# Gate and residual for the first half of an output projection, and gates stored tile by tile

## The chip, the cores and the metric

The kernel runs on one core of a Trainium2 chip. The metric is the time of one execution on the device, in microseconds (us). The kernel before took 3386.41 us, the median of three runs from 3386.09 to 3387.73.

## The reference

One step of a diffusion backbone with two kinds of linear recurrence side by side, in fp32. There are 2048 latent tokens (a grid of 64 columns and 32 rows) and 128 context tokens, of 1024 features each.

```python
def _layer(x, mod, st_a, st_b, p, grid_rows):
    sh1, sc1, g1, sh2, sc2, g2 = split(mod)
    h = rms_norm(x, norm1) * (1 + sc1) + sh1
    # group A, HGRN2 in raster order; group B, gated DeltaNet in column order
    o_a = head_rms_norm(oa_f + flip(oa_b)) * silu(a_g)
    o_b = head_rms_norm(ob_f + flip(ob_b)) * silu(b_z)
    y = concat([o_a, o_b]) @ w_out          # (tokens, 1024) x (1024, 1024)
    x = x + g1 * y                          # g1 is one row for latent, one for context tokens
    h = rms_norm(x, norm2) * (1 + sc2) + sh2
    return x + g2 * ((silu(h @ w_gate) * (h @ w_up)) @ w_down), states
```

Since `concat([o_a, o_b]) @ w_out` is a sum of two products, `x + g1 * y` can be taken as `(x + g1 * (o_a @ w_a)) + g1 * (o_b @ w_b)` or as `x + g1 * (o_a @ w_a + o_b @ w_b)`.

## The kernel before

Tokens are handled in 17 tiles of 128: 16 of latent tokens, in column order of the grid, and one of the context (index `NL`). fp32 products are made of three products of split halves (`oh`, `ol` and `woh`, `wol`). The stages come in this order: norm and transposes; the input projections, the short convolution and the two sigmoid gates; the HGRN scan; the preparation of the gated DeltaNet scan; the gated DeltaNet scan itself, with the output projection worked into it; the FFN.

Four pieces of work matter here.

*The gates.* `gate_block` (L268 to L280) computes one head's gate for all 2176 tokens, with the head's 128 features on partitions, in one tile `ct`, and stores it to `gate_d` in DRAM. There are eight such blocks, four heads for each of the two groups. `out_a` (L790) loads back one tile's gates of four heads (L802).

*The triangular inverse.* For the DeltaNet scan a 128x128 triangular matrix of each tile and head is inverted: 32x32 blocks on VectorE and GpSimd, and then two levels on TensorE, in `A3` (L650 to L705). One tile's levels are a chain of small matmuls (L675, L681, L686, L696, L701) with copies on ScalarE and VectorE between them. The result lies in one of two buffers `XT` and is stored by L705. The latent tiles come first, the context tile last. The memory of these work tiles is given back when the last tile is done, and later ones (`g1c` among them) are laid out over it.

*The scan.* `scan` (L914) takes one tile in one direction: matmuls `pkS`, `pv`, `pS`, `po`, `pa`, of which each depends on the one before through VectorE or ScalarE. 34 steps are run, 16 latent tiles and the context in both directions. `scan_load` (L886) and `scan_pre` (L898, whose product is `pqk`, L905) prepare a step.

*The output projection.* It is made in two parts: part 0 is the HGRN group's share, for which everything is there early, part 1 the DeltaNet group's, for which a tile must have been passed by both directions of the scan. For each tile and part `out_a` norms the heads, transposes them (L820) and applies the gate (L821 to L823); `out_b` (L826) makes two halves of 512 output features, each with 12 matmuls into a PSUM tile `py` (L847), of which there are two. In part 0 the half is copied (L855) and the sum parked in DRAM (`xa_d`, L857). In part 1 it is added to what was parked (L851, VectorE), multiplied by the gate row `gm` (L852, GpSimd), added to the residual x (L853, GpSimd) and stored to `x2_d` (L859). The gate row is `g1`, held all the time, for latent tiles, and `g1c`, loaded when needed, for the context tile (L836). `out_step` calls both one after the other for each tile; part 0 begins with the context tile, part 1 takes it among its first tiles.

The order of instructions on each engine is not that of the source. A scheduler that simulates a timeline fixes it when the program is built (`schedule_with_timeline_sim=True`), so each engine has a static order, and an instruction that must wait holds back all that stand behind it on its engine. All DMAs are issued by SyncE (SP), also in one static order.

Of the kernel before, what the change touches and what calls it, by code (L numbers as in the profile page):

```python
# [24 lines left out]
H = 4  # L25
# [8 lines left out]
def hybrid_step(ctx: ExitStack, tc, x, vecs, ada1, ada2, bada, win, wgt, alog, dtb, sa, sb, wout, wg, wu, wd, normf,  # L34
# [19 lines left out]
    def scr(shape, name):  # L54
        return drm.tile(shape, F32, tag=name, name=name)


    qkv_d = scr([NT, P, 4, H, P], "qkvd")
    gate_d = [scr([P, H, TOK], f"gated{i}") for i in range(2)]
    oa_d = scr([TOK, H, P], "oad")  # L60
    mod_d = scr([2, 4 * D], "modd")
    gr_d = scr([2, NT * H, P], "grd")
# [205 lines left out]
    def gate_block(b):  # L268
        w = load_w(win[16 + b if b < H else 32 + b - H])
        ct = gq.tile([P, TOK], F32, tag="gct", name="gct")  # L270
        for i, (c0, n) in enumerate(PIECES):
            pj = proj(w, i)
            r0, r1 = lat_rows(i)
            nl = (r1 - r0) * GW
            nc.scalar.activation(out=colmajor(ct[:, 0:LAT])[:, r0:r1, :],
                                 in_=pj[:, 0:nl].rearrange("p (r c) -> p r c", c=GW), func=AF.Copy)
            if nl < n * P:
                nc.scalar.activation(out=ct[:, LAT:TOK], in_=pj[:, nl:n * P], func=AF.Copy)
        nc.scalar.activation(out=ct, in_=ct, func=AF.Silu)
        dma(out=gate_d[b // H][:, b % H, :], in_=ct)  # L280


    with sB:
# [470 lines left out]
    def rows_of(src, c, w):  # L754
        return src[0:LAT].rearrange("(r w) f -> w r f", w=GW)[4 * c + w]
# [34 lines left out]
    def out_a(c, part, ob):  # L790

        o4 = ob
        if part == 0:
            o4 = wk5.tile([P, H, P], F32, tag="o4", name="o4", bufs=3)
            oaf = oa_d.rearrange("t h v -> t (h v)")
            if c == NL:
                dma(out=o4.rearrange("p h v -> p (h v)"), in_=oaf[LAT:TOK])
            else:
                for w in range(4):
                    dma(out=o4[32 * w:32 * w + 32].rearrange("p h v -> p (h v)"), in_=rows_of(oaf, c, w))  # L800
        gt = wk5.tile([P, H, P], F32, tag="gt5", name="gt5", bufs=3)
        dma(out=gt, in_=gate_d[part][:, :, c * P:(c + 1) * P])  # L802
        sq = wk5.tile([P, 3, H], F32, tag="sq5", name="sq5", bufs=10)
        jk = wk5.tile([P, P], F32, tag="jk5", name="jk5")
        for h in range(H):
            nc.scalar.activation(out=jk, in_=o4[:, h], func=AF.Square, accum_out=sq[:, 0, h:h + 1])  # L806
        if part == 0:
            nc.vector.tensor_scalar(out=sq[:, 0], in0=sq[:, 0], scalar1=1.0 / P, scalar2=EPS, op0=ALU.mult,
                                    op1=ALU.add)
        else:  # L810
            nc.vector.scalar_tensor_tensor(out=sq[:, 0], in0=sq[:, 0], scalar=1.0 / P, in1=nq2[:, c],
                                           op0=ALU.mult, op1=ALU.add)
        rsqrt(sq[:, 1], sq[:, 0], sq[:, 2])
        for h in range(H):
            nc.scalar.activation(out=o4[:, h], in_=o4[:, h], func=AF.Copy, scale=sq[:, 1, h:h + 1])
        oh = wk5.tile([P, H, P], F32R, tag="oh", name="oh", bufs=2)
        ol = wk5.tile([P, H, P], F32R, tag="ol", name="ol", bufs=2)
        pt = ps5.tile([P, H, P], F32, tag="ot", name="ot")
        for j in range(H):
            nc.tensor.transpose(pt[:, j], o4[:, j], ident)  # L820
        nc.vector.tensor_tensor(out=gt, in0=pt, in1=gt, op=ALU.mult)  # L821
        nc.scalar.activation(out=oh, in_=gt, func=AF.Copy)
        nc.vector.tensor_tensor(out=ol, in0=gt, in1=oh, op=ALU.subtract)  # L823
        return oh, ol

    def out_b(c, part, oh, ol):  # L826

        xt = wk5.tile([P, D], F32, tag="xt5", name="xt5", bufs=2)
        gm = g1
        if part:  # L830
            x2 = wk5.tile([P, D], F32, tag="x2", name="x2", bufs=2)
            dma(out=xt, in_=xa_d[c])
            if c == NL:
                dma(out=x2, in_=x[LAT:TOK])
                gm = wk6.tile([P, D], F32, tag="h2", name="g1c")
                dma(out=gm, in_=mod_d[1:2, 0:D].broadcast_to([P, D]))  # L836
            else:
                for w in range(4):
                    dma(out=x2[32 * w:32 * w + 32], in_=rows_of(x, c, w))
        woh, wol = wos[part]  # L840
        for n in range(2):
            cs = slice(512 * n, 512 * n + 512)
# [2 lines left out]
            for k in range(H):  # L845
                for a, b in ((oh, woh), (oh, wol), (ol, woh)):
                    nc.tensor.matmul(out=py, lhsT=a[:, k], rhs=b[:, k, cs], start=t == 0,  # L847
                                     stop=t == 3 * H - 1)
                    t += 1
            if part:  # L850
                nc.vector.tensor_tensor(out=xt[:, cs], in0=py, in1=xt[:, cs], op=ALU.add)  # L851
                nc.gpsimd.tensor_tensor(out=xt[:, cs], in0=xt[:, cs], in1=gm[:, cs], op=ALU.mult)  # L852
                nc.gpsimd.tensor_tensor(out=x2[:, cs], in0=x2[:, cs], in1=xt[:, cs], op=ALU.add)  # L853
            else:
                nc.vector.tensor_copy(out=xt[:, cs], in_=py)  # L855
        if not part:
            dma(out=xa_d[c], in_=xt)  # L857
            return None
        dma(out=x2_d[c], in_=x2)  # L859
        return x2  # L860

    def norm_T(c, xt, h2, r, bank):

# [526 lines left out]
```

## Time and profile before

| What | Value |
|---|---|
| Median of three runs | 3386.41 us |
| The profiled execution: its time, its span | 3381.0 us, 3379.1 us |
| Mean granted TensorE clock in it | 0.965 |
| Busy: PE, DVE, ACT, POOL | 3148.7, 1877.4, 1388.1, 987.8 us |
| Levels of the inverse (L650 to L705) end | 1463 us after the span's start |
| Projection part 0, matmuls | 1325 to 1533 us |
| Projection part 1, matmuls of latent tiles | 1619 to 1833 us |
| First FFN matmul (L1169) | 1846 us |

Times of the trace are counted from the span's start. "Busy" is the time in which an engine had an instruction running; overlapping matmuls are counted once in a stretch's busy time, while the groups of the same matmuls add up their durations. "PEclk" is the clock granted to TensorE as a share of full speed. A wait is put down to the engine and instruction that released it last.

### The profile page before, as it was taken

The page shows a single profiled execution, that of the slowest core. Times are in us where ns is not written, and L with a number is a line of the kernel's source. Part 1 is how long each engine was busy: PE and PEld are TensorE (multiplying, and loading weights), DVE is VectorE, ACT ScalarE, POOL GpSimd, SP SyncE. Part 2 cuts the span into 40 slices and gives each one's busy share as a digit, 9 for nine tenths or more (in the row PEclk, how much of TensorE's full clock was granted, in tenths as well). Part 3 has the DMA queues.
Part 4 walks back from the last instruction along what each step waited for, and adds up shares of the span by engine and source line. Part 5 has one row for each costly group of instructions (what it writes and reads, how often), then busy time and mean ns, then how long its engine had stood idle before and what let it go on. Part 6 is the DMA issues. An engine that isn't in the chain of part 4 may idle for free.

```text
span 3379.1 us, 50825 instructions
## 1 busy us (share of the span) xinstructions
PE 3148.7 (93%) x18712; PEld 2815.3 (83%) x18712; DVE 1877.4 (56%) x3702; ACT 1388.1 (41%) x2993; POOL 987.8 (29%) x1006
## 2 busy tenths in 40 slices
PE   7899979999999889998886999998999999999997
PEld 4687779999998777878775888987999998899996
DVE  4667744474563864665666777778233337333336
ACT  6455435364474534763753545543111113211111
POOL 1100001121122327413566444456111114211114
PEclk8999999999999988999998999998999999999998
DMA  5234410111115667867775888988656666666553
GB/s 219 71 111 142 116 54 29 53 47 36 49 42 150 170 171 247 275 226 264 250 243 168 343 339 334 352 342 322 223 192 218 218 210 233 248 218 218 208 200 116
DMA packets 325241, 647.85 MB, mean 192 GB/s; under 512 B 77178, under 2 KB 177314, under 8 KB 310146
## 3 DMA queue, kind: packets, MB, share of 16 engines
q1 hardware_dynamic: 324994, 644.61, 56.2%
q8 instruction: 148, 2.42, 0.3%
q14 instruction: 99, 0.81, 0.1%
HBM read 446.23 MB, written 198.28 MB: 191 GB/s over the span
## 4 chain that ended last, share of the span: by engine, by line
PE 43%; DVE 6%; DMA 5%; ACT 3%; POOL 2%; issue 2%; SPq 0%; POOLq 0%; DVEq 0%; ACTq 0%
PE z L1169 23%; PE y L1252 12%; PE py L847 3%; PE pS L938 1%; PE pj L257 1%; DVE wp L1067 1%; DMA e<-grd 1%; PE pa L954 1%; DMA wr<-in_wu_dram 1%; DVE acc L1204 1%; DMA x<-in_x_dram 1%; PE po L947 0%; DVE acc L1257 0%; POOL s L1070 0%; ACT jk L806 0%
## 5 line engine op out<-in xcount | busy, mean ns | idle before, releaser
L257 PE MATMUL pj<-hh,wh 128*128 128x384 f32 (+2 forms) x1480 | 546.9, 370 | 14.3 <-DVE q L464 7.0
L257 PE MATMUL pj<-hl,wh 128*128 128x384 f32 (+2 forms) x1480 | 545.9, 369 | 0.4 <-POOL hl L231 0.3
L257 PE MATMUL pj<-hh,wl 128*128 128x384 f32 (+2 forms) x1480 | 545.6, 369 | 0.0
L1316 POOL TENSOR_TENSOR u<-u,g 128x384 f32<-128x384 f32 (+1 forms) x132 | 135.9, 1031 | 779.0 <-DVE u L1177 758.5
L1257 DVE TENSOR_TENSOR acc<-y,acc 128x512 f32<-128x512 f32 x328 | 223.9, 688 | 251.4 <-PE y L1252 250.8
L257 PEld LDWEIGHTS pj<-hh,wh 128*128 128x128 f32 (+1 forms) x1480 | 281.1, 190 | 46.6 <-DVE q L464 7.2
L257 PEld LDWEIGHTS pj<-hl,wh 128*128 128x128 f32 (+1 forms) x1480 | 280.7, 190 | 29.9 <-issue 3.3
L257 PEld LDWEIGHTS pj<-hh,wl 128*128 128x128 f32 (+1 forms) x1480 | 280.6, 190 | 28.0 <-issue 2.3
L1252 PE MATMUL y<-wd,hid0h 128*128 128x512 f32 x748 | 237.7, 400 | 19.7 <-DVE acc L1257 7.2
L1252 PE MATMUL y<-wd,hid1h 128*128 128x512 f32 x748 | 236.6, 397 | 0.8 <-DMA wd<-wdd 0.8
L1295 ACT ACTIVATE g<-g 128x384 f32<-128x384 f32 (+1 forms) x132 | 66.6, 507 | 288.5 <-DVE g L1177 288.4
L494 POOL TENSOR_SCALAR th<-th,nlbh,lbh 128x384 f32<-128x384 f32 (+1 forms) x40 | 61.2, 1530 | 405.7 <-ACT G L492 401.8
L1252 PEld LDWEIGHTS y<-wd,hid0h 128*128 128x128 f32 x748 | 137.5, 190 | 41.7 <-DVE acc L1257 9.3
L1252 PEld LDWEIGHTS y<-wd,hid1h 128*128 128x128 f32 x748 | 140.8, 189 | 32.5 <-issue 1.2
L1177 DVE TENSOR_TENSOR g<-z,g 128x384 f32<-128x384 f32 (+1 forms) x165 | 85.1, 533 | 146.7 <-PE z L1169 146.1
L1169 PE MATMUL z<-x1h,wp 128*128 128x384 f32 (+1 forms) x528 | 143.7, 335 | 17.9 <-ACT wp L1066 13.2
L1169 PE MATMUL z<-x6h,wp 128*128 128x384 f32 (+1 forms) x528 | 145.9, 334 | 14.2 <-ACT wp L1066 8.6
L1177 DVE TENSOR_TENSOR u<-z,u 128x384 f32<-128x384 f32 (+1 forms) x165 | 84.9, 531 | 117.9 <-PE z L1169 117.5
L1252 PE MATMUL y<-wd,hid1l 128*128 128x512 f32 x374 | 147.4, 397 | 1.7 <-POOL hid1l L1067 1.7
L1252 PE MATMUL y<-wd,hid0l 128*128 128x512 f32 x374 | 148.0, 399 | 0.0
L1066 ACT ACTIVATE hid1h<-u 128x384 fp32r<-128x384 f32 (+3 forms) x77 | 34.2, 458 | 267.7 <-POOL u L1316 267.7
L1169 PE MATMUL z<-x2h,wp 128*128 128x384 f32 (+1 forms) x528 | 140.8, 329 | 1.1 <-DMA wp<-wpd 1.1
(373 smaller groups left out, 7904.6 us busy)
## 6 DMA issues: line engine op xcount, KB each, us to landing
wp<-wpd SPq DMA_DIRECT2D x308, 512.0 KB
wpd<-wp SPq DMA_DIRECT2D x154, 512.0 KB
wd<-wdd SPq DMA_DIRECT2D x44, 1024.0 KB
ld<-qkvd SPq DMA_DIRECT2D x34, 1024.0 KB
wdd<-wd SPq DMA_DIRECT2D x22, 1024.0 KB
raw<-in_win_dram SPq DMA_DIRECT2D x72, 256.0 KB
e<-grd SPq DMA_DIRECT2D x68, 256.0 KB
at<-in_ada_dram SPq DMA_DIRECT2D x64, 256.0 KB
```

The source lines that it names most:

```text
L257: nc.tensor.matmul(out=out, lhsT=a[:, k], rhs=b[:, k], start=t == 0, stop=t == 3 * KD - 1)
L494: nc.gpsimd.tensor_scalar(out=th, in0=th, scalar1=nlbh[:, col:col + 1], scalar2=lbh[:, col:col + 1], op0=ALU.mult, op1=ALU.add)
L847: nc.tensor.matmul(out=py, lhsT=a[:, k], rhs=b[:, k, cs], start=t == 0, stop=t == 3 * H - 1)
L938: nc.tensor.matmul(out=pS[:, h], lhsT=kn[:, h], rhs=vv[:, h], start=True, stop=True)
L954: last[0] = nc.tensor.matmul(out=pa[:, h], lhsT=at[:, h], rhs=vv[:, h], start=True, stop=True)
L1066: nc.scalar.activation(out=wh, in_=raw, func=AF.Copy)
L1169: nc.tensor.matmul(out=z, lhsT=w_[:, k], rhs=x_[:, k, :N], start=t == 0, stop=t == 3 * HK - 1)
L1177: nc.vector.tensor_tensor(out=out, in0=z, in1=b, op=ALU.add)
L1252: nc.tensor.matmul(out=py, lhsT=u_[:, o:o + P], rhs=v_[:, cs], start=t == 0, stop=t == 5)
L1257: nc.vector.tensor_tensor(out=acc[c][:, cs], in0=py, in1=acc[c][:, cs], op=ALU.add)
L1295: nc.scalar.activation(out=g, in_=g, func=AF.Silu)
L1316: nc.gpsimd.tensor_tensor(out=us[i], in0=us[i], in1=gs[i], op=ALU.mult)
```

## The change

Two things are changed. The gates are stored as one block for each tile (`gate_d` has the tile as its first index): the store of a gate block writes 17 pieces of 512 bytes for each partition in place of one row of 8.7 KB, and the load of a tile's gates reads one piece of 2 KB in place of four of 512 bytes. And `out_b` does in both parts what it did in neither before: it multiplies the half by the gate row straight out of PSUM (VectorE) and adds to it (GpSimd) what stands in `xt`, which is the residual x in part 0 and the parked sum in part 1.

```diff
-    gate_d = [scr([P, H, TOK], f"gated{i}") for i in range(2)]
+    gate_d = [scr([NT, P, H, P], f"gated{i}") for i in range(2)]
...
-        dma(out=gate_d[b // H][:, b % H, :], in_=ct)
+        dma(out=gate_d[b // H][:, :, b % H, :].rearrange("c p t -> p c t"), in_=ct.rearrange("p (c t) -> p c t", t=P))
...
-        dma(out=gt, in_=gate_d[part][:, :, c * P:(c + 1) * P])
+        dma(out=gt, in_=gate_d[part][c])
...
     def out_b(c, part, oh, ol):
 
         xt = wk5.tile([P, D], F32, tag="xt5", name="xt5", bufs=2)
+        x2 = wk5.tile([P, D], F32, tag="x2", name="x2", bufs=2)
         gm = g1
+        if c == NL:
+            gm = wk6.tile([P, D], F32, tag="h2", name="g1c")
+            dma(out=gm, in_=mod_d[1:2, 0:D].broadcast_to([P, D]))
         if part:
-            x2 = wk5.tile([P, D], F32, tag="x2", name="x2", bufs=2)
             dma(out=xt, in_=xa_d[c])
-            if c == NL:
-                dma(out=x2, in_=x[LAT:TOK])
-                gm = wk6.tile([P, D], F32, tag="h2", name="g1c")
-                dma(out=gm, in_=mod_d[1:2, 0:D].broadcast_to([P, D]))
-            else:
-                for w in range(4):
-                    dma(out=x2[32 * w:32 * w + 32], in_=rows_of(x, c, w))
+        elif c == NL:
+            dma(out=xt, in_=x[LAT:TOK])
+        else:
+            for w in range(4):
+                dma(out=xt[32 * w:32 * w + 32], in_=rows_of(x, c, w))
...
-            if part:
-                nc.vector.tensor_tensor(out=xt[:, cs], in0=py, in1=xt[:, cs], op=ALU.add)
-                nc.gpsimd.tensor_tensor(out=xt[:, cs], in0=xt[:, cs], in1=gm[:, cs], op=ALU.mult)
-                nc.gpsimd.tensor_tensor(out=x2[:, cs], in0=x2[:, cs], in1=xt[:, cs], op=ALU.add)
-            else:
-                nc.vector.tensor_copy(out=xt[:, cs], in_=py)
-        if not part:
-            dma(out=xa_d[c], in_=xt)
-            return None
-        dma(out=x2_d[c], in_=x2)
-        return x2
+            nc.vector.tensor_tensor(out=x2[:, cs], in0=py, in1=gm[:, cs], op=ALU.mult)
+            nc.gpsimd.tensor_tensor(out=x2[:, cs], in0=x2[:, cs], in1=xt[:, cs], op=ALU.add)
+        dma(out=(xa_d, x2_d)[part][c], in_=x2)
+        return x2 if part else None
```

The change also moves instructions on every engine. Lines behind L826 differ between the two files: L847, L905, L927, L933 and L889 of before are L848, L899, L921, L927 and L883 of after.

On PE, in the middle of the inverse's levels. `pl` and `pn` are the levels' products (L675 to L701), `py` the projection's, `pqk`, `pkS` and `pa` the scan's. Before:

```order
L847 MATMUL py<-woh,ol 128x512
L701 MATMUL pl_10429<-kTa 64x64 x8
L681 MATMUL pl_10462<-NS,dd 32x32 x16
L847 MATMUL py<-woh,oh 128x512
L847 MATMUL py<-wol,oh 128x512
```

After, at the same levels:

```order
L820 MATMUL ot<-ident,o_12405 128x128 x4
L696 MATMUL pl_10429<-XT_8657,e 64x64 x8
L675 MATMUL pl_10462<-dd,L 32x32 x16
L899 MATMUL pqk<-ld 128x128 x4
L948 MATMUL pa<-vv,e 128x128 x4
L921 MATMUL pkS<-S_12833,ld 128x128
L701 MATMUL pl_10429<-kTa 64x64 x8
L681 MATMUL pl_10462<-NS,dd 32x32 x16
L921 MATMUL pkS<-S_12833,ld 128x128 x3
L686 MATMUL pn_10496<-dd,NS 32x32 x4
```

Between the context tile's two halves and the last level, before has 18 further halves of `py` (216 matmuls), after none; before has come to 14 tiles of L820 by the last level, after to 7. Both have done six scan steps by then. Behind the last level, the halves of part 0 that are left stand among five scan steps before, and 34 halves among seven after; the steps that follow up to the twentieth, nine before and seven after, have no projection beside them in either.

On SP, where the levels end. `xtd` is the store of a tile's inverse, `XT<-xtd` the scan's load of it, `g1c` the context's gate row, `wor` weights of the output projection, `xad` the parked sum. Before:

```order
L705 DMA xtd<-XT_8656 128x1024
L800 DMA o_14468<-oad 32x512
L892 DMA XT<-xtd 128x512 x3
L836 DMA g1c<-modd 128x1024
L892 DMA XT<-xtd 128x512
L783 DMA wor<-in_wout_dram 128x1024
L857 DMA xad_12203<-xt_13255 128x1024
```

After:

```order
L705 DMA xtd<-XT_8656 128x1024
L705 DMA xtd<-XT_8657 128x1024
L705 DMA xtd<-XT_8656 128x1024
L833 DMA g1c<-modd 128x1024
L886 DMA XT<-xtd 128x512 x3
L833 DMA g1c<-modd 128x1024
L886 DMA XT<-xtd 128x512
L853 DMA xad_12216<-x_12370 128x1024
L840 DMA xt_12510<-in_x_dram 32x1024 x4
```

The first load of the gate row stands at the same place as the only one before, behind the store of the last tile's inverse; a second one follows for part 1. Of the parked sums nine (the first of them far ahead of these rows) are stored before that place in the kernel before, and none in the kernel after.

On DVE, at the same place of the kernel after. L704 and L690 end a tile's levels, and `g1c` is read by the first output of the projection:

```order
L704 COPY XT_8657<-pl_10921 64x4x64 x2
L690 COPY XT_8656<-pl_10954 32x4x32 x4
L688 COPY NS<-pn_10988 32x4x32 x2
L704 COPY XT_8656<-pl_11003 64x4x64 x2
L923 SCALAR_TENSOR_TENSOR ld<-pkS,nrg,ld 128x128 x4
L851 TENSOR_TENSOR x_12370<-py,g1c 128x512 x2
L851 TENSOR_TENSOR x_12440<-py,g_12282 128x512 x2
```

Before, the copies of L855 that take their place stand among the levels of eight tiles, the first of them behind L820 of the third tile.

## Rows read from the trace of the kernel before

**Rows 1.** The page, parts 1 and 4: busy us (share) xinstructions; chain by engine.

```profile
span 3379.1 us, 50825 instructions
PE 3148.7 (93%) x18712; PEld 2815.3 (83%) x18712; DVE 1877.4 (56%) x3702; ACT 1388.1 (41%) x2993; POOL 987.8 (29%) x1006
...
PE 43%; DVE 6%; DMA 5%; ACT 3%; POOL 2%; issue 2%; SPq 0%; POOLq 0%; DVEq 0%; ACTq 0%
```

**Rows 2.** Windows: us; PE, PEld, DVE, ACT, POOL busy; PEclk; DMA; GB/s.

```profile
1333.00:1463.00 130.00, 125.39 (x1342) 107.71 (x1341) 77.12 (x218) 86.99 (x281) 54.75 (x91) 0.96 0.83 273
1463.00:1610.00 147.00, 127.29 (x832) 113.98 (x829) 75.42 (x191) 68.93 (x187) 42.22 (x46) 0.95 0.76 255
1540.00:1610.00 70.00, 56.09 (x439) 53.75 (x438) 35.86 (x107) 32.59 (x94) 26.98 (x30) 0.95 0.82 278
1612.00:1818.00 206.00, 185.17 (x1131) 159.76 (x1130) 138.93 (x355) 129.30 (x374) 121.48 (x104) 0.97 0.71 229
1818.00:1846.00 28.00, 10.82 (x28) 7.40 (x28) 22.59 (x22) 10.02 (x21) 22.68 (x15) 0.68 0.37 131
```

**Rows 3.** PE groups from 1330 to 1465: shapes xcount | busy us, mean ns.

```profile
L847 PE MATMUL py<-woh,oh 128*128 128x512 f32 x76 | 31.1, 409 | 0.0
L820 PE MATMUL ot<-ident,o 128*128 128x128 f32 x48 | 7.7, 277 | 0.0
```

**Rows 4.** L847, two halves: ns, first and last start of every third matmul.

```profile
L847 PE MATMUL py<-woh,oh x8: 390/394/479, 1405.7 to 1410.7; 128*128 128x512 f32 x8
```

**Rows 5.** SP's issue of the context gate, L836.

```profile
L836 SPq DMA_DIRECT2D g1c<-modd x1: 319/319/319, 1470.6 to 1470.6; - x1
```

**Rows 6.** SP: stores of the level results, L705.

```profile
L705 SPq DMA_DIRECT2D xtd<-XT x11: 320/377/1818, 1302.9 to 1466.2; - x11
```

**Rows 7.** Two neighbouring tiles in the levels, L696.

```profile
L696 PE MATMUL pl<-XT,e x16: 218/218/313, 1301.6 to 1302.3; 64*64 64x64 f32 x16
L696 PE MATMUL pl<-XT,L x16: 311/311/365, 1310.0 to 1311.3; 64*64 64x64 f32 x16
```

**Rows 8.** The scan steps without projection, L938 (8 matmuls each).

```profile
L938 PE MATMUL pS<-vv,ld x72: 275/275/582, 1548.1 to 1611.3; 128*128 128x128 f32 x72
```

**Rows 9.** DMA from 1333 to 1463.

```profile
DMA packets 28782, 35.44 MB, mean 273 GB/s; under 512 B 12288, under 2 KB 20621, under 8 KB 27609
```

**Rows 10.** PE's waits from 1612 to 1818.

```profile
PE pS L938 <- ACT vv L935: 7.6, 8, 3.0
PE ot L820 <- POOL x L853: 4.2, 3, 1.9
PE nt L870 <- DVE h L873: 2.3, 2, 1.9
PE py L847 <- ACT oh L822: 1.8, 2, 1.2
PE ot L820 <- POOL xt L852: 1.3, 1, 1.3
```

**Rows 11.** POOL groups from 1612 to 1840.

```profile
L852 POOL TENSOR_TENSOR xt<-xt,g 128x512 f32<-128x512 f32 x32 | 41.8, 1308 | 40.5 <-DVE xt L851 14.9 <-DVE sq L127 6.8 <-DVE sq L131 6.3
L853 POOL TENSOR_TENSOR x<-x,xt 128x512 f32<-128x512 f32 x32 | 41.5, 1300 | 6.7 <-PE ot L820 2.2 <-DMA x<-in_x_dram 1.8 <-PE py L847 0.8
```

**Rows 12.** DVE: L823 from 1465 to 1541, without additions on POOL.

```profile
L823 DVE TENSOR_TENSOR ol<-gt,oh 128x512 fp32r<-128x512 f32 x6 | 4.1, 686 | 0.7 <-ACT oh L822 0.7
```

**Rows 13.** DVE: L823 and L128 from 1612 to 1834, beside them.

```profile
L823 DVE TENSOR_TENSOR ol<-gt,oh 128x512 fp32r<-128x512 f32 x16 | 12.8, 803 | 0.9 <-ACT oh L822 0.9
...
L128 DVE TENSOR_TENSOR sq<-sq 128x4 f32<-128x4 f32 (+1 forms) x19 | 9.1, 480 | 0.4
```

**Rows 14.** Windows within one store: 512 B pieces, then 8.7 KB rows.

```profile
301.00:303.00 2.00, 2.00 (x13) 2.00 (x12) 0.69 (x1) 1.87 (x11) 0.00 (x0) 1.00 1.05 291
...
1071.00:1073.00 2.00, 1.15 (x9) 0.76 (x8) 0.00 (x0) 1.44 (x6) 1.64 (x2) 1.00 1.08 442
```

**Rows 15.** PE's waits from 1818 to 1850.

```profile
PE z L1169 <- ACT wp L1066: 13.2, 1, 13.2
```

## The prediction

> **What bounds the kernel now.** I read the page first. PE is busy for 3148.7 of the span's 3379.1 us, and the chain that ended last lies more on PE than on anything else [rows 1]. So the kernel is bound by how densely PE's work stands in its static order, and time is won or lost only where PE stands idle. I then cut the stretch that the change touches into windows [rows 2]. From 1333 to 1463 us, while the inverse's levels run, PE is busy for 125.4 of 130 us: the small matmuls of the levels are chains of waits, and projection and scan fill their gaps. From 1463 to 1610 us PE has 127.3 of 147, and in its second part, where only scan steps are left, 56.1 of 70. The nine steps there start their `pS` from 1548.1 to 1609.7 us or so (72 matmuls in nine groups of eight, the last at 1611.3 [rows 8]), 7.7 us each. In part 1 (1612 to 1818) PE has 185.2 of 206. The waits of PE there name GpSimd's L852 and L853 and what comes late through ScalarE and VectorE [rows 10]. Last come 28 us with 10.8 of PE, which end with a wait of 13.2 us for the FFN's first weights [rows 2, 15].
>
> **The change, part by part.** The sum is made against the profiled execution, 3381.0 us with 1.9 us around its span; it is 5.4 us under the median of 3386.4 us, and I add that at the end.
>
> *Work is kept, and moved.* 34 copies and 34 additions on VectorE become 68 multiplications that also read one PSUM and one SBUF tile. GpSimd keeps 68 operations, of which 34 move from part 1 to part 0; each took 1.30 us [rows 11]. The 8.9 MB of x are now read in part 0. Only the second load of `g1c` is new, 0.5 MB.
>
> *Term 1, the levels.* This is the part of the change that its text does not tell. In part 0 the first half of the projection now needs the gate row of the context. Its load stood at 1470.6 us, directly behind the last store of the inverse at 1466.2 [rows 5, 6], and stands at the same place after; but before, part 0 did not ask for it. With two PSUM tiles for `py`, no third half can be made until then, and the order on PE shows just that: the 18 halves are gone from between the levels, and with them 7 tiles of L820. One half is 12 matmuls; the 24 of two halves ran from 1405.7 to 1411.5 at 0.238 us each (21 steps in 5.0 us [rows 4]), so 2.85 us a half and 51 us for 18. The other two thirds of the 229 recorded matmuls have rows like the one in [rows 3]. Seven tiles of L820 are 28 transposes at most 0.28 us apart [rows 3] and overlapped; I take half, 4 us. So PE loses 55 of its 125 us of work, and 70 are left. How far does the stretch shrink? Three things hold it up. The chain of one tile, unfilled, took 8.4 us (1301.6 to 1310.0 [rows 7]); eight tiles make 67. Six scan steps at 7.7 make 46 beside them; run one after the other with the levels that would be 113. And the DMAs moved 35.4 MB here at 273 GB/s [rows 9]; without nine parked sums, two weight loads and the inputs of seven tiles (10 MB) about 26 MB are left, 95 us at this rate. The last three stores of the inverse stand back to back, with nothing beside them on SP. I take 100 us, a little above the DMAs' 95, since both chains share one in-order PE: −30. Bounds: −60 (only the 70 us of PE's work count) and 0 (SP and the two chains hold it where it was).
>
> *Term 2, the work comes back.* The 55 us stand behind the levels. The first output waits for `g1c` and the x tiles behind it on SP: +3 (0 to +6). Seven scan-only steps in place of nine leave PE two times less idle; nine had 13.9 us [rows 2], so −3. 34 additions of GpSimd now run beside this part. They were seen to slow VectorE: L823 took 686 ns without them and 803 beside them, and the little operations of L128 took 480 ns on average there [rows 12, 13]. Most of that hides behind 34 dense halves; +2 (0 to +10). DMA is no bound: 37.5 MB of this stretch (147 us at 255 GB/s) and 10.5 more in some 203 us are 236 GB/s, less than the 273 seen before. Sum +57, bounds +48 to +70.
>
> The Trainium skill, "SBUF — State Buffer", section "Who interferes with whom", says that VectorE with two inputs in SBUF and GpSimd reading SBUF share a port pair, which one holds for a whole instruction while the other is fully blocked. The rows agree: an operation of four elements lasted as long as a good part of an addition. By this rule the blocking moves into part 0 with the 34 additions and leaves part 1 by as much, and the new multiplication, with only one input in SBUF, is not touched; the sum stays what it is.
>
> *Term 3, part 1.* Each tile loses two of four operations on GpSimd and 512 KB of x loads in SP's queue. PE's 5.5 us of waits for L852 and L853 should go, and half of the 11.7 us for L935, L873 and L822, which are late through blocked VectorE or a late `ld` [rows 10]: −11. Bounds 0 (a scan step's own latency takes their place) and −21 (all idle time of the stretch [rows 2]).
>
> *Term 4, the end.* The last two halves pass one operation of GpSimd in place of two: −2.6, bounds −4 and 0, since the 13.2 us of waiting for the FFN's weights [rows 15] are mostly these weights' own.
>
> *Term 5, the gate layout.* Eight stores become pieces of 512 B. A store of the same size with such pieces ran at 291 GB/s, the row-wise one at 442 [rows 14]; 1.11 MB take 3.8 in place of 2.5 us. That makes 10 us of DMA time, while PE works on the next block; the 34 loads gain about as much. I take 0, bounds −3 and +10. The Trainium skill, "DMA: Bandwidth & Descriptors", section "Specifications", puts line rate at pieces of 512 B and up, by which the store would cost nothing more; the trace does not agree, with 291 beside 442 GB/s. By either the sum is the same.
>
> Sum: −30 + 57 − 11 − 2.6 + 0 = +13, so 3394 us for an execution like the profiled one and 3399 us on the median's footing.
>
> **The rivals.**
>
> *Faster: the levels close up.* If steps and levels overlap well and the DMAs run as fast as within one store, 291 to 442 GB/s [rows 14], the stretch falls to its 72 us of PE's work: −58 + 56 − 14 − 3 = −19, and 3367 us. For it: the levels need little DMA. Against it: 26 MB in 72 us are 360 GB/s, where 273 was the mean.
>
> *No change.* The stretch falls to 88 us and part 1 gains a little more: −42 + 56 − 13 − 2 = −1, about 3385 us. For it: work is only moved. Against it: moved from where PE's gaps are to where they are fewer.
>
> *Much slower.* Scan steps and levels run one after the other on PE's in-order queue, 113 us, and wait for loads behind a blocked SP besides, 120: −10 + 60 − 8 − 2 = +40, about 3426 us. What decides is where the last level ends: behind 1448 us this is the case. For it: 4.6 us of idle time were all that the fillers left, so latency of the chains was hidden and its real size is not seen.
>
> *The change does not do what it says:* if blocked GpSimd or VectorE keep part 1 at its 13.7 us a step (206 us for 15 steps), term 3 is 0 and the time 3410 us. This lies inside the forecast's own bounds.
>
> **How the numbers follow.** What a measurement of this kernel can tell from no change is about 0.2%, 7 us. Forecast and its neighbours (3393 to 3412 us): 0.38. Much slower: 0.12. No change: 0.20. Faster: 0.30; it has so much because every term's bound below is far from what I took. Slower is therefore 0.50, same 0.20, faster 0.30. The likeliest case alone reaches from 3390 to 3414 us; the range for 8 times in 10 takes in the faster case and most of the much slower one, 3364 to 3426 us.
>
> **What would show it.** In the profile after: no `py` between about 1333 us and the last L701, whose end I expect near 1433 us (right between 1420 and 1448; below 1410 the faster rival, above it the slower one). The first multiplication with `g1c` about 3 us later, and PE waiting there for DMA or VectorE. Scan-only steps of 7.7 us, seven of them. The first projection matmul of a latent tile in part 1 near 1646 us in place of 1619. Part 1 at 13.0 us a step in place of 13.7, with GpSimd's L852 named less often by PE's waits. L823 slower than 686 ns in the dense part, nearer to 690 in part 1. A gate store at about 290 GB/s. The forecast is wrong if this matmul comes before 1630 us, or if part 1 keeps its step.

## The result and the profile after

The changed kernel took 3422.22 us, the median of four runs from 3420.36 to 3423.36, beside 3386.25 us for the kernel before (four runs, 3384.17 to 3387.73): slower by 36 us, or 1.0106 by these eight times. The ratio on record is 1.0119, with a 95% interval from 1.0100 to 1.0139 that holds both. The forecast had 3399 us, slower by 13: the direction was right, the size was not.

The two profiled executions differ by 42.4 us of span (3379.1 and 3421.5). I cut both at the same points of the program:

| Stretch, from PE's matmuls | Before, us | After, us | Difference | Forecast |
|---|---|---|---|---|
| to the first of the projection | 1325.3 | 1329.1 | +3.8 | 0 |
| on to the last of the levels (L701) | 137.8 | 116.4 | −21.4 | −30 |
| on to the twentieth scan step | 146.6 | 209.7 | +63.1 | +57 |
| on to the 34th scan step (part 1) | 199.0 | 199.0 | 0.0 | −11 |
| on to the FFN's first | 37.5 | 36.1 | −1.4 | −2.6 |
| the FFN's | 1518.9 | 1518.1 | −0.8 | 0 |

The rows add up to 43.3 us; the tail behind the FFN's last matmul was 0.9 us shorter after. The forecast's terms add up to +13.4. A scan step is counted from its first `pS`. The cuts are read from the first and last starts of a line's instructions. Of the kernel after: the last levels, the loads of the context's gate row (two now), the scan steps up to the twentieth, and the FFN's first group.

```profile
L701 PE MATMUL pl<-NS x64: 218/218/365, 1364.6 to 1445.5; 64*64 64x64 f32 x64
...
L833 SPq DMA_DIRECT2D g1c<-modd x2: 319/319/319, 1449.6 to 1455.2; - x2
...
L932 PE MATMUL pS<-vv,ld x60: 275/275/553, 1596.3 to 1656.8; 128*128 128x128 f32 x60
...
L1163 PE MATMUL z<-x1h,wp x528: 302/334/689, 1890.2 to 3349.1; 128*128 128x384 f32 x117, 128*128 128x320 f32 x59
```

The gate row is asked for 21 us earlier than before [rows 5], because the levels end 18 us earlier, and the twentieth step's last `pS` comes at 1656.8 in place of 1611.3 [rows 8]. What was won in the levels is lost three times over behind them.

The windows of the kernel after that answer to [rows 2] (same columns; the cuts are those of the table):

```profile
1329.00:1445.00 116.00, 89.34 (x1156) 80.02 (x1154) 58.02 (x170) 69.74 (x220) 58.32 (x99) 0.83 0.81 250
1445.00:1655.00 210.00, 182.13 (x1063) 157.38 (x1060) 103.97 (x249) 89.16 (x255) 82.51 (x74) 0.94 0.80 256
1655.00:1854.00 199.00, 180.33 (x1100) 158.27 (x1100) 129.92 (x344) 127.27 (x363) 83.60 (x75) 0.95 0.57 195
...
1863.00:1892.00 29.00, 11.80 (x31) 7.98 (x31) 22.20 (x21) 12.35 (x27) 21.08 (x14) 0.67 0.37 134
```

In the levels PE is idle for 27 us, where 4.6 us were idle before, and the granted clock is 0.83 in place of 0.96. In part 1 the columns of GpSimd and of the DMAs show the relief that was made: GpSimd down from 121 of 206 us to 84 of 199, DMA from 0.71 to 0.57. PE's columns show that it bought nothing.

PE's waits of the kernel after, first in the levels (1336 to 1446):

```profile
PE pqk L899 <- DMA ld<-qkvd: 7.0, 1, 7.0
PE pkS L921 <- ACT of L957: 5.1, 1, 5.1
PE ot L820 <- ACT o L815: 4.8, 2, 3.6
PE pl L696 <- ACT XT L668: 2.7, 4, 1.5
```

behind them (1446 to 1594):

```profile
PE py L848 <- DVE x L851: 7.8, 5, 3.6
PE pv L927 <- DMA XT<-xtd: 2.4, 1, 2.4
```

and in part 1 (1655 to 1854):

```profile
PE pS L932 <- ACT vv L929: 14.6, 9, 4.4
PE nt L864 <- ACT x L858: 4.6, 3, 2.3
PE py L848 <- ACT oh L822: 1.5, 3, 0.9
PE ot L820 <- POOL x L852: 0.7, 1, 0.7
```

The waits for GpSimd's L852 and L853 were 5.5 us [rows 10] and are 0.7. In their place stands the wait for `vv`, a copy on ScalarE. ScalarE's timeline of the kernel after shows what stood ahead of one such wait of 2.74 us (start, length, instruction; `pv` was done by 1747.7; the last line is PE's):

```profile
1748.17 1.28 ACT L898 ACT_TABLE_LOAD   x1
1749.46 1.28 ACT L898 ACTIVATE e<-e,nG 128x128 f32<-128x128 f32 x4
1750.65 0.57 ACT L929 ACTIVATE vv<-pv 128x512 f32<-128x512 f32 x1
1751.27 0.94 PE L932 MATMUL pS<-vv,ld 128*128 128x128 f32 x6 [2.74 <-ACT vv L929]
```

ScalarE does not wait here; it is busy with the next step's exponentials, and the table load for them, which stand ahead of `vv` in its static order. In the kernel before they stood there too, ahead of a wait of 2.98 us:

```profile
1709.30 1.28 ACT L904 ACT_TABLE_LOAD   x1 [0.29 <-DMA e<-grd]
1711.33 1.28 ACT L904 ACTIVATE e<-e,nG 128x128 f32<-128x128 f32 x4 [0.74 <-POOL e L900]
1712.51 0.58 ACT L935 ACTIVATE vv<-pv 128x512 f32<-128x512 f32 x1
1713.14 1.16 PE L938 MATMUL pS<-vv,ld 128*128 128x128 f32 x8 [2.98 <-ACT vv L935]
```

There 0.74 us of ScalarE's time were a wait for GpSimd, so before the change a part of this delay came from GpSimd after all.

### The profile page after: what moved, and what is told of

Read it like the earlier page. It is cut to its first block, busy times and chain, and to the rows that moved or that the text cites. A ratio compares the mean times of both kernels' runs of the same rounds, so it can differ in the third digit from the quotient of the medians.

```text
span 3421.5 us, 50857 instructions
## 1 busy us (share of the span) xinstructions
PE 3160.7 (92%) x18712; PEld 2824.5 (83%) x18712; DVE 1873.7 (55%) x3702; ACT 1390.7 (41%) x2995; POOL 987.4 (29%) x1006
## 4 chain that ended last, share of the span: by engine, by line
PE 39%; DVE 6%; ACT 4%; DMA 3%; issue 3%; POOL 3%; SPq 0%; POOLq 0%; DVEq 0%; ACTq 0%
PE z L1163 23%; PE y L1246 11%; PE py L848 2%; DMA wr<-in_wu_dram 1%; PE pS L932 1%; POOL s L1064 1%; DVE acc L1251 1%; ACT L126 1%; DVE acc L1198 1%; DVE wp L1061 0%; ACT jk L806 0%; POOL u L1310 0%; DMA wor<-in_wout_dram 0%; PE po L941 0%; DMA xt<-in_x_dram 0%
## 5 line engine op out<-in xcount | busy, mean ns | idle before, releaser
L257 PE MATMUL pj<-hh,wh 128*128 128x384 f32 (+2 forms) x1480 | 547.1, 370 | 13.3 <-DVE q L464 6.9
L1246 PEld LDWEIGHTS y<-wd,hid0h 128*128 128x128 f32 x748 | 137.3, 189 | 43.3 <-DVE acc L1251 9.9
L1163 PE MATMUL z<-x7h,wp 128*128 128x384 f32 (+1 forms) x528 | 140.9, 330 | 1.7 <-ACT wp L1060 1.6
```

The costliest lines, as they stand in the source:

```text
L257: nc.tensor.matmul(out=out, lhsT=a[:, k], rhs=b[:, k], start=t == 0, stop=t == 3 * KD - 1)
L1163: nc.tensor.matmul(out=z, lhsT=w_[:, k], rhs=x_[:, k, :N], start=t == 0, stop=t == 3 * HK - 1)
L1246: nc.tensor.matmul(out=py, lhsT=u_[:, o:o + P], rhs=v_[:, cs], start=t == 0, stop=t == 5)
```

## The experiments

The theory after the result (A): what the change costs is the wait for the context's gate row, which keeps 18 halves out of the levels. Its rivals: the additions and x loads that came into part 0 (B), and the gate layout. Ratios are to the kernel before on the same chip; its own runs there spread from 3374 to 3394 us, so the intervals matter more than the medians.

**The context tile alone.** The kernel before, with the new path for the context tile and no other:

```diff
+        new = c == NL
...
+            if new:
+                nc.vector.tensor_tensor(out=x2[:, cs], in0=py, in1=gm[:, cs], op=ALU.mult)
+                nc.gpsimd.tensor_tensor(out=x2[:, cs], in0=x2[:, cs], in1=xt[:, cs], op=ALU.add)
-            if part:
+            elif part:
```

> The kernel before (old layout, copies in part 0, addition, multiplication and addition in part 1), except that the context tile alone is handled as in the changed kernel: multiplied by its gate row in part 0 already. So 32 of 34 halves are as before, but the wait for the row is there; the static order has 2 halves between the levels. Theory A: the levels end near 1446 us, the twentieth scan step comes near 1650 us, and the time is 3412 to 3424 us. Theory B: 3385 to 3392 us.

Measured 1.0104 (1.0092 to 1.0117). One tile of 17 gives nearly the whole loss. Its two windows up to the last level and to the twentieth step:

```profile
1324.00:1444.00 120.00, 94.57 (x1160) 83.93 (x1157) 57.46 (x171) 69.98 (x220) 58.31 (x99) 0.79 0.74 235
1444.00:1645.00 201.00, 179.65 (x1056) 156.10 (x1055) 102.91 (x249) 90.27 (x256) 40.38 (x42) 0.95 0.70 234
```

The pattern is that of the changed kernel, with only two additions of part 0 on GpSimd. Theory A holds for this kernel; B is not needed for most of the loss.

**The latent tiles alone**, its counterpart (`new = c != NL`, old layout):

> The counterpart of the run in which the context tile alone was handled as in the changed kernel (1.0104 of before): here the 16 latent tiles get gate and residual in part 0, and the context tile goes the old way, with the old layout of the gates. No half of part 0 waits for the context's gate row; 18 halves stand between the levels. Theory A (the wait is the loss): 0.999 to 1.003 of before. Theory G (moving the additions and loads of 32 halves costs about a third of the loss too, as the kernel with the row in its own tile left 1.0056): 1.003 to 1.006.

Measured 1.0038 (1.0024 to 1.0052): the likelier of the two readings was G. There is a smaller loss in moving the latent tiles' work. It does not add to the wait: the change with the old layout, which has both, stood at 1.0094.

**The row in its own tile.** The changed kernel, and as a control the kernel before, with

```diff
     g1 = wa.tile([P, D], F32, tag="g1", name="g1")
+    g1x = wa.tile([P, D], F32, tag="g1x", name="g1x")
...
             dma(out=g1, in_=mod_d[0:1, 0:D].broadcast_to([P, D]))
+            dma(out=g1x, in_=mod_d[1:2, 0:D].broadcast_to([P, D]))
...
-            gm = wk6.tile([P, D], F32, tag="h2", name="g1c")
-            dma(out=gm, in_=mod_d[1:2, 0:D].broadcast_to([P, D]))
+            gm = g1x
```

> The changed kernel, with one difference: the context's gate row lies in a tile of its own, in memory that nothing else uses, and is loaded together with the latent gate row long before the levels of the inverse end. Its static order has about 22 halves of the projection between the levels again, in place of 2. Theory A (the wait for this row, which keeps the projection out of the levels, is what the change costs): the last level ends near 1463 us again, the twentieth scan step comes near 1612 us, and the time is 3378 to 3394 us. Theory B (the additions on GpSimd and the loads of x, now in part 0, cost it): 3410 us or more. If the relief of part 1 is real once part 0 is mended, it is under 3380 us.

> A control: the kernel before, with the context's gate row in a tile of its own, loaded with the latent one, and nothing else changed; 20 halves stand between the levels as before. Theory G: 0.999 to 1.001, and what the kernel with the own tile left of the loss belongs to gate and residual in part 0. Theory F (the own tile itself moves memory and the schedule): 1.003 to 1.005.

Measured 1.0056 (1.0038 to 1.0073) and, for the control, 1.0020 (1.0010 to 1.0031). The repair takes back about half of the loss, less than theory A said, though 22 halves stand between the levels again: the last level came at 1479.9 us in place of the 1463 expected, the twentieth step 16 us late as well, and the stages behind them took as long as before. By this profile, what is left of the loss lies in the stretch of the levels. The control lies between its two theories: the own tile, with a load at another place, costs by itself. The rest can be put down to the tile, the layout and the latent tiles' work (0.0020, 0.0012 and 0.0038); added up they come to 0.0070, somewhat more than the 0.0056, and no run shows that they add.

**The context tile last** in part 0 (`halves[0][1:] + halves[1] + [NL]`):

> The changed kernel with the context tile as the last of part 0 in place of the first, so that its row is asked for when the levels are over anyway. 23 halves and 5 scan steps stand between the levels. Theory A: 1.000 to 1.006 of before. If the wait were not the cause, 1.010 or more.

Measured 1.0061 (1.0043 to 1.0079), at the upper end of what A said. Twice, taking the wait away by another route took back half.

**The layout**, by itself and taken out of the change:

> The kernel before with the gates stored tile by tile, and nothing else changed. Theory A with the 3.8 us by which the changed kernel was late at its first projection matmul put down to the layout: 3388 to 3392 us. Rival: the layout is hidden behind PE, 3384 to 3388 us, and the 3.8 us come from somewhere else. If the layout carried most of the loss it would be over 3400 us.

> The changed kernel with the old layout of the gates, so gate and residual in both parts alone. Theory A: the loss stays, 3414 to 3422 us, and the first projection matmul comes near 1325 us as before. If the layout carried most of it: under 3400 us.

Measured 1.0012 (1.0000 to 1.0023) and 1.0094 (1.0076 to 1.0112). The layout is worth some 4 us against the kernel, by an interval that begins at 0. It does not explain the 3.8 us at the first projection matmul: the layout alone had that matmul at 1325.5, and a kernel that differs from before only in the scan (vv on VectorE, below) had it at 1328.6. That is how far one execution's stretch strays. What a store costs is seen in two windows of the changed kernel, each within one store, with hardly a packet of anything else:

```profile
1142.00:1144.00 2.00, 2.00 (x11) 1.73 (x10) 1.90 (x5) 0.72 (x4) 0.75 (x1) 1.00 1.11 334
...
1239.00:1241.00 2.00, 2.00 (x10) 1.65 (x10) 1.90 (x6) 0.00 (x0) 0.00 (x0) 1.00 1.05 304
```

Other such windows lie between 290 and 348 GB/s. The one of 442 in [rows 14] also counts other loads' pieces of 2 KB; a window of the kernel before with hardly anything but the 8.7 KB rows (1137 to 1139 us) had 418.

**What the latent tiles' part costs.** Three kernels take from part 0 the x loads (`xt = g1`, so the residual is left out), the additions (8 columns in place of 512), or, with the latent tiles alone on the new path, both:

```diff
-            nc.gpsimd.tensor_tensor(out=x2[:, cs], in0=x2[:, cs], in1=xt[:, cs], op=ALU.add)
+            sm = cs if part else slice(512 * n, 512 * n + 8)
+            nc.gpsimd.tensor_tensor(out=x2[:, sm], in0=x2[:, sm], in1=xt[:, sm], op=ALU.add)
```

> The kernel with the context's gate row in its own tile, without the loads of x in part 0: GpSimd adds the resident latent gate row in place of x, so the additions stay and 8.9 MB of loads go (the residual is left out of the result). That kernel stood at 1.0056 of before, with its levels stretch 22 us longer than before while the DMAs moved 42.8 MB at 267 GB/s, where before moved 37.8 MB at 274. Theory C (the levels stretch is paced by its DMAs, and the x loads put 5 MB into it): the stretch from the first projection matmul to the last level falls from 160 to 135 to 145 us, and the time to 0.996 to 1.003 of before. Theory D (the 34 additions on GpSimd beside VectorE's and ScalarE's small operations hold it up): no change, 1.004 to 1.007.

> The kernel with the context's gate row in its own tile, with the loads of x in part 0 kept and the additions of part 0 cut from 512 to 8 columns (so most of x is left out of the result). Theory C (DMAs): the stretch of the levels stays near 160 us and the time at 1.004 to 1.007 of before. Theory D (additions): the stretch falls to 140 us or so, and the time to 0.998 to 1.003.

> The kernel in which the latent tiles alone are handled as in the change (1.0038 of before), with both of what that moves into part 0 taken away: the resident gate row in place of the loads of x, and additions of 8 columns. The multiplication in place of the copy stays. If additions and loads together carry what is left of the loss: 0.997 to 1.001. If the order of instructions carries it: 1.002 to 1.005.

Measured 1.0055 (1.0043 to 1.0067) without the loads and 1.0037 (1.0024 to 1.0050) with small additions, both beside 1.0056; and 0.9990 (0.9977 to 1.0002) with both away, beside 1.0038. Theory C fell: without 4.4 MB of loads the stretch of the levels was no shorter (164.9 us beside 159.9). Theory D is not shown either: the interval reaches into both, and the stretch stayed at 160.5 us where D said 140. With both away the 0.0038 are gone, but not by these two alone as far as is shown: that kernel's static order has some 25 halves between the levels, where its counterpart has 18. Whether the order or the pair carries the 0.0038, and how the pair shares it, stays open.

**Why part 1 gave nothing back.** First, the other half of GpSimd's work cut away in part 1 as well (8 columns):

> The kernel with the context's gate row in its own tile, with the additions of part 1 cut from 512 to 8 columns (most of what was parked is left out of the result). Term 3 of the prediction expected 11 us from taking half of GpSimd's work off part 1, and none came: 199 us of fourteen steps in both kernels. If GpSimd does not bound part 1, it stays at 196 to 203 us without the other half too, and the time at 1.003 to 1.007 of before. If it does, the stretch falls below 193 us.

Measured 1.0045 (1.0031 to 1.0058), and 202.5 us for the fourteen steps. GpSimd busy for 54 of 202 us instead of 84 made no difference, and PE's first wait was the same (its window of part 1, and the first line of PE's waits there):

```profile
1630.00:1832.00 202.00, 181.62 (x1096) 159.69 (x1097) 123.58 (x344) 127.23 (x362) 53.56 (x75) 0.94 0.56 193
```

```profile
PE pS L934 <- ACT vv L931: 12.4, 9, 2.7
```

Then that copy was put on VectorE, in the kernel before, in the changed kernel, with the latent tiles alone, and with one of GpSimd's operations cut:

```diff
-        nc.scalar.activation(out=vv, in_=pv, func=AF.Copy)
+        nc.vector.tensor_copy(out=vv, in_=pv)
```

> The kernel before, with one copy of each scan step (vv out of PSUM, 0.57 us) on VectorE in place of ScalarE. In part 1 PE's largest wait, before and after, is for this copy, which stands behind the next step's four exponentials and their table load in ScalarE's order. Theory E (this order, not GpSimd, sets part 1's step): these waits go, the fourteen steps fall from 199 to 188 to 195 us and the time to 0.995 to 0.999 of before. Rival: VectorE, busy for 134 of these 199 us, holds the copy back as long, or PE's own work is the step: 0.999 to 1.005.

> The changed kernel, whole, with the copy vv on VectorE and nothing else different. Theory H (part 1's relief was there, but hidden: ScalarE's order held vv back, and with it off ScalarE the halved work of GpSimd and SP counts): the fourteen steps of part 1 take 183 to 190 us in place of 199, and the time is 0.994 to 0.997 of the changed kernel's 1.0119, so 1.006 to 1.009 of before. Rival: only the 2 to 4 us that vv alone gave: part 1 at 195 to 200 us, 1.0085 to 1.0115.

> The version that the runs point to: latent tiles handled as in the change, context tile as before, old layout, and the copy vv on VectorE, which by itself gave 0.9983 of before. If the relief of part 1 shows once ScalarE's order is out of the way, 0.994 to 0.998; if the two only add, with the latent tiles at 1.000 to 1.004: 0.998 to 1.003.

> The kernel before with the copy vv on VectorE and GpSimd's multiplication of part 1 cut from 512 to 8 columns (the gate is left out for the rest), so that one full operation for each half is left, while the x loads stay in part 1. Theory H with GpSimd as the second bound: part 1 at 184 to 191 us, 0.994 to 0.997 of before. If the loads of x in SP's queue are the second bound: part 1 stays near 197 us, 0.997 to 0.9995.

| Kernel | Ratio (interval) | Part 1, 14 steps, us |
|---|---|---|
| before, `vv` on VectorE | 0.9983 (0.9973 to 0.9993) | 197.0 |
| change, `vv` on VectorE | 1.0104 (1.0087 to 1.0121) | 190.5 |
| latent tiles alone, `vv` on VectorE | 0.9980 (0.9969 to 0.9992) | 185.7 |
| before, `vv` on VectorE, one GpSimd operation cut | 0.9937 (0.9924 to 0.9950) | 191.3 |

Windows of part 1, in the order of the rows:

```profile
1609.00:1806.00 197.00, 179.24 (x1101) 155.36 (x1102) 143.72 (x359) 121.53 (x356) 118.23 (x102) 0.96 0.73 235
```

```profile
1652.00:1843.00 191.00, 176.73 (x1102) 153.51 (x1103) 137.03 (x360) 119.66 (x354) 83.06 (x75) 0.97 0.60 207
```

```profile
1615.00:1801.00 186.00, 172.69 (x1100) 149.49 (x1101) 139.13 (x360) 119.21 (x353) 83.89 (x75) 1.00 0.63 212
```

```profile
1607.00:1798.50 191.50, 173.59 (x1095) 153.28 (x1096) 133.04 (x359) 121.39 (x356) 87.49 (x101) 0.97 0.75 242
```

In the first of these kernels the waits for `vv` are nearly gone, and another wait, for VectorE's `ld`, has come up:

```profile
PE pv L933 <- DVE ld L929: 6.3, 2, 4.5
...
PE pS L938 <- DVE vv L935: 0.9, 1, 0.9
```

So its time is where theory E had it, and its 197.0 us are not (188 to 195).

With `vv` on ScalarE, part 1 took 199.0 to 205.7 us in four kernels with the old part 1, and 198.1 to 204.6 in eight with the relieved one: means of 202.9 and 200.4. With `vv` on VectorE it took 197.0 with the old and 185.7 to 191.3 in three with a relieved one (mean 189.2). So two things are shown. The relief alone is worth no more than these executions stray. And with the relief made, moving `vv` took 8.5 and 16.7 us off part 1 (199.0 to 190.5 in the changed kernel, 202.4 to 185.7 with the latent tiles alone): ScalarE's order was what PE waited for.

Theory H says more: two bounds, one behind the other, of which the change moved the hidden one. It fits, and is not settled. For it, the latent tiles' 1.0038 and the 0.9983 of `vv` would add up to 1.0021, and together they measured 0.9980, on the border between what H and the plain sum had been given. Against it, in the changed kernel the time fell from 1.0119 (1.0106 by the listed runs) to 1.0104, no more than `vv` gives alone, while its part 1 fell by 8.5 us to half a microsecond above what H said. And the old part 1 with `vv` on VectorE is a single execution, where executions with the same part 1 stray by up to 6.7 us.

Which of GpSimd's work and the x loads comes second stays open as well. The last row cuts GpSimd's work and leaves the x loads, and its ratio is clearly below the first row's. But in its part 1 PE is idle for 17.9 us, as in the first row (17.8), beside 14.3 and 13.3 in the two kernels that also moved the x loads; what it gained there is busy time of PE. And of the 15.2 us between the profiled executions of the first and the last row only 7.6 lie in part 1 and behind it up to the FFN, 6.0 in the FFN, which the cut does not touch.

The version that beats both kernels is the third row, 0.9980, or simply `vv` on VectorE, 0.9983; between them no difference is shown. The last row leaves part of the gate out and is no version.

## Why the prediction was wrong

*Term 3 failed.* It read the waits for L852 and L853 (5.5 us) and half of those for L935, L873 and L822 as time that returns: −11. It came out as 0.0, and by the means above as little more than −2. Part 1 kept its step, 14.2 us in both profiles, which the prediction had named as a sign that it is wrong. The first half of the claim was right, the waits for GpSimd went from 5.5 to 0.7 us. But PE then waited for `vv`. I had put half of L935's 7.6 us down to a late `ld` or a blocked VectorE, and had not looked at what stood ahead of `vv` on ScalarE: four exponentials and a table load, there before and after. The bound for 0 in the term, "a scan step's own latency takes their place", was nearly the right rival, and came true. The 0 was also one of the rivals, at 3410 us.

*Term 1 was mis-sized*, −21.4 for −30. The place was right: no `py` between the second half and the last level, whose end (1445.5) fell into the 1420 to 1448 that I had called right, though near its edge. The work taken out was right too. PE's busy time in the stretch went from 133.2 to 89.7 us, at clocks of 0.96 and 0.83: 53 us less of work at full speed, and the 55 us forecast are 53 at the 0.96 of before. What I left out is the clock, which goes between two levels in these traces, 0.5 and 1.0 of full speed. The levels' small matmuls, without the dense fillers, ran at 0.83 in the mean, and the same 74 us of full-speed work took 90 in place of 78. This is an estimate from busy times and mean clocks, not an experiment on the clock. The traces bear it out: four kernels have the same 1156 matmuls in this stretch, PE was busy with them for 89.7 to 94.5 us, and its busy time at the upper level plus half of that at the lower comes to 76 us in each. The idle 27 us, about what the forecast had, lie mostly on ScalarE and on the scan's loads; the DMAs at 250 GB/s were a little under the 273 taken.

*Term 2 was a little small*, +63.1 for +57. PE's busy time rose by 54.8 us (55 forecast). The rest is idle time of PE: 8.3 us more than before, where I had counted +2 in all. Three windows of the stretch show where it stood, the start, the dense part with the start in it, and the scan-only steps:

```profile
1446.00:1456.00 10.00, 5.49 (x22) 4.93 (x23) 3.15 (x8) 0.00 (x0) 1.33 (x2) 0.50 0.52 184
...
1446.00:1594.00 148.00, 133.75 (x692) 112.06 (x692) 72.30 (x158) 61.57 (x176) 59.89 (x51) 0.93 0.79 249
1594.00:1655.00 61.00, 47.60 (x360) 44.73 (x360) 31.57 (x91) 27.59 (x80) 22.62 (x24) 0.97 0.83 278
```

`g1c` landed some 4 us after its issue, and 10 us passed from the last level to the first dense halves. The scan-only steps left PE idle for 13.4 us, hardly less than the nine of before (13.9), so the −3 did not come. And PE waited 7.8 us for L851, some 6.4 of them in two waits that are not L851's own. There it stands in VectorE's order behind the split of an output weight (L788), which waits for ScalarE's share of it, and that for the weight's load:

```profile
1549.30 1.59 DVE L788 SCALAR_TENSOR_TENSOR wol<-wor,vec,woh 128x1024 fp32r<-128x1024 f32 x1 [3.78 <-ACT woh L787]
1550.82 0.68 DVE L851 TENSOR_TENSOR x<-py,g 128x512 f32<-128x512 f32 x1
```

*Term 4* gave −1.4 for −2.6. *Term 5*, the layout, was 0 inside bounds of −3 and +10; alone it measured about +4 (its interval begins at 0). The store ran at 304 and 334 GB/s, a little better than the 291 taken. By the Trainium skill, "DMA: Bandwidth & Descriptors", section "Specifications", nothing should have been lost, and the trace still disagrees, though by less.

By the rule of the Trainium skill on the shared port pair ("SBUF — State Buffer", section "Who interferes with whom") blocking was to move into part 0 with the additions, and the traces do not single that out. L823 took 774 ns on average behind the levels (686 before in [rows 12]), but it took 770 there in the kernel with the context tile alone too, which has hardly an addition there; the split L788, also with two inputs in SBUF, took 1424 ns beside the additions and 1286 in that kernel. In part 1 L823 took 817 ns (803 before); over all kernels with `vv` on ScalarE it took 758 to 803 ns with the old part 1 and 755 to 817 with a relieved one, so that the blocking "leaves part 1 by as much" is not borne out by it. That the multiplication is untouched agrees: L851, with one input in SBUF in either kernel, took 686 ns in both.

Of the rivals, *much slower* gave the size (3426 us for 3422), and not for its reason: the levels did not take 120 us. The forecast's shortfall of 30 us, between the profiled executions, lies in part 1's missing 11 us, in the levels (8.6, the clock), behind them (6.1), in the end (1.2), and in 3.8 us ahead of the projection, which is no more than these executions stray. That the measured time lies inside the range of 3364 to 3426 us is owed to the width of that range.

## What to carry to other kernels

When an operation is moved to an earlier stage, look first at what it needs that the stage did not need before, and where that lies in memory: here one row of 4 KB per partition, laid out over an earlier stage's tiles, cost 35 us where it was the only thing changed, and it showed in the static order before any run. A wait listed as "PE waits for X" is worth its time only if nothing else ends just behind it; ask what the releaser's engine would have been doing, in its own order. And dense fillers between chains of small matmuls went with a higher clock here as well as with a higher busy share, so taking them out gave back less than their own time, 21 us for some 53.

## What was not expected of the hardware

In a stretch with PE busy for 77% of the time, in small matmuls, the granted clock was 0.83 (0.79 in the kernel with the context tile alone), beside 0.96 when the same chains were filled with 128x512 matmuls. All seventeen kernels fall apart in this way: with 2 halves between the levels four had 0.79 to 0.83, and with 18 or more thirteen had 0.90 to 0.98.

Part 1 ran at 1.00 in the fastest of its stretches (the latent tiles alone with `vv` on VectorE, 186 us), beside 0.93 to 0.97 in the sixteen others, and PE's busy time was 172.7 us there, beside 179.6 in the kernel before, with the same matmuls. That is half of what this stage won. It came in one profiled execution, and the other three kernels with `vv` on VectorE had 0.96 and 0.97, so it is not shown that a `vv` done sooner raises the clock.
